# A normalisation of queries and keys that covers two tiles at a time, with its weight applied on ScalarE

## The chip, the cores and the metric

The kernel runs on one core of a Trainium2 chip. The metric is the device time of one execution in microseconds (us); less is better. The median of three runs before the change is 1447.38 us.

## The reference

One encoder layer on 1024 tokens of width 1024: a dilated window attention in three groups of eight heads beside a gated linear recurrence, each behind a gate, then projections and a residual. What matters here is the input projection of the queries and keys and their norm over each head's 64 channels:

```
h = rms_norm(x, norm_w)
z = h @ w_in                                     # [1024, columns], float32
q = rms_norm(qkv_a[:, :, g, 0], q_norm_w[g])     # per token and head, over 64 channels
k = rms_norm(qkv_a[:, :, g, 1], k_norm_w[g])
rms_norm(t, w) = t * rsqrt(mean(t * t, axis=-1) + EPS) * w
```

q and k have 1024 tokens x 3 groups x 8 heads x 64 channels. After it, each group gathers keys and queries by stride (1, 4 or 16 tokens) and does a banded softmax attention.

## The kernel before

**Precision and products.** Each float32 product is three matmuls in a reduced float type on TensorE (PE): operands are split into a rounded high part and a low remainder (`whi`, `wlo` for weights; `hh`, `hl` and the sums `S0h` to `S3l` for the activations), and high x high, low x high and high x low are added in one PSUM bank. ScalarE (ACT) makes the high part, GpSimd (POOL) or VectorE (DVE) the low one.

**Stages.** First the u and v projections (to about 142 us), then the stage this is about, the "blocks" (to about 681 us), then attention, merge, recurrence and output.

**A block.** A block multiplies 256 columns of weights (1024 rows, as four raw tiles of 128 x 512) with all 1024 tokens, by a scheme of seven products instead of eight (`run_quads`, line 449). Its steps, in order, are 11, T1, T2, 21, T3, (11 of the next block), 22, T4; each is 12 matmuls of 128 x 512. Three PSUM banks per block are named `qA` (11, then T2, T3 and T4 added onto it), `qE` (T1, 22) and `qC` (21). Partial results are copied out by ACT: p behind 11, c behind T1, u behind T2; DVE then adds: p is whole behind 21, c behind T3, u behind 22, and the fourth tile is copied behind T4. T3 writes to the bank that u is copied from, so PE can't begin T3 before ACT has copied u. Of the 27 blocks 12 are "qk" blocks, four in each group; they come in pairs, with other blocks (gates, q of the recurrence) between. For a qk block p, c, u and the fourth tile lie in the ring `spare` (7 buffers), for others in `stage`. A tile is 128 channels by 512 tokens; p and u are one half of the tokens, c and the fourth tile the other.

**Rings.** A ring's `get` hands out its buffers in turn; if the next is still in use, the emission first runs waiting tasks until it is free (line 544). The norm has `ny` (4 buffers), `nhi` and `nlo` (2 each); raw weights have `qraw` (6).

**The norm of a tile** (lines 1130 to 1182). As soon as a tile is whole: ACT squares it (`ny`) and copies the square to `nhi`; DVE makes `nlo`; PE sums over the channels of a head with a block matrix of ones (`headones`), two matmuls into a bank `nss`; ACT does Ln, Exp and Square; DVE does three steps in one task (`newton`): a correction from `nss`, the tile times its weight `nqk` and the estimate, and their product, written in the order of the group's stride; then the spare is free, and SP stores the tile to DRAM (`qkD`). 48 tiles, so 96 matmuls. A tile holds two heads of 64 channels.

**What sets the order.** Each engine executes its instructions in program order. That order is made while the program is built: class Plan (line 132) keeps an estimated clock for each engine and each buffer, and class Builder emits a waiting task (`tick`) or a norm product (`burst`) once its inputs are estimated to be there and its ring has room; products of the norm may stand only between two steps. All instructions go through one helper, so every row of the profile has line 58; rows are told apart by tile names. Loads and stores are issued by SP, in its program's order.

Of the kernel before, what the change touches and what calls it, by code (L numbers as in the profile page):

```python
# [8 lines left out]
F32 = mybir.dt.float32  # L9
# [3 lines left out]
AF = mybir.ActivationFunctionType  # L13
# [17 lines left out]
QRAW, SPARE = 6, 7  # L31
LOWS = ("T2", "T4")
# [194 lines left out]
class Builder:  # L227
# [176 lines left out]
    def start_quads(self, ring):  # L404
# [219 lines left out]
def hybrid_block(ctx, tc, a, out):  # L624
# [50 lines left out]
    def block_pages(kind, *at):  # L675
# [11 lines left out]
        return tuple(_dram(wi, (p + 4 * k) * 65536 + 128 * (2 * e + col), [[512, 128], [65536, 4], [1, 128]])  # L687
# [21 lines left out]
    consts.tile([128, 48], F32, name="pad")  # L709
    eps = consts.tile([128, 1], F32, name="eps")  # L710
    half_ones = consts.tile([128, 2], F32, name="half_ones")
    v_.memset(eps, EPS)
    v_.memset(half_ones, 0.0)
    for j in range(2):
        v_.memset(half_ones[64 * j:64 * j + 64, j:j + 1], 1.0)
# [106 lines left out]
    nqk = consts.tile([128, 6], F32, name="nqk")  # L822
# [10 lines left out]
    def bias_tables(p):  # L833
        g_.tensor_scalar(nqk[:, 0:3], nqk[:, 0:3], -0.125 / 128.0, None, op0=OP.mult)
        g_.tensor_scalar(nqk[:, 3:6], nqk[:, 3:6], -1.0 / 128.0, None, op0=OP.mult)
# [155 lines left out]
    for d in range(8):  # L991
# [4 lines left out]
        if d == 3:  # L996
            s_.dma_start(nqk, a["qk_w"])
# [97 lines left out]
    def blocks_start():  # L1095

        if "p" in blk or blk["n"] < 16:
# [13 lines left out]
        v_.tensor_copy(blk["ones"].rearrange("p (j c) -> p j c", j=2),  # L1111
                       half_ones[:, :, None].to_broadcast([128, 2, 64]))
# [1378 lines left out]
```

## Time and profile before

| what | value |
|---|---|
| runs | 1447.38 us (median), 1442.25 and 1447.64 |
| profiled execution | 1447.14 us, span in the profile 1445.4 us |
| granted TensorE clock | 0.999 |
| busy share | PE 99%, DVE 66%, ACT 62%, POOL 24% |
| DMA | 230.52 MB, mean 159 GB/s |

A row of a timeline gives the start in us from the span's beginning, the duration, the engine, the operation with the tiles it writes and reads (`out<-in`), and in brackets how long the engine was idle before it and what released it. A row of a group gives the count, the shortest, median and longest duration in ns, and first and last start. Rows with SPq are DMA issues: the duration there is the issue's.

### The profile page before, as it was taken

Reading aid. Unit: us, or ns where it says so; the run is one execution under the profiler, and the core shown is the slowest. Engines: PE = TensorE matmul, PEld = TensorE weight load, DVE = VectorE, ACT = ScalarE, POOL = GpSimd, SP = SyncE. Lnnn points to the kernel's source line nnn. Section 1 sums busy time; section 2 is a strip of 40 time slices with the busy share of each in tenths; the row PEclk is TensorE's granted clock in tenths of the full one; section 3 lists DMA queues with packets and bytes.
Section 4 is the critical chain, followed back from the end, with each engine's and each line's share of the span. In section 5 each row is a group of like instructions: output and inputs, shape, how many; then the busy total and the mean of one; then the engine's idle time right before and its main releaser. Section 6 shows DMA issues by size and latency. Waiting matters only on the chain. (4 is left out here: it accounts for less than half of the span.)

```text
span 1445.4 us, 23404 instructions
## 1 busy us (share of the span) xinstructions
PE 1430.0 (99%) x8154; PEld 1188.0 (82%) x8154; DVE 959.4 (66%) x1905; ACT 889.0 (62%) x1897; POOL 340.5 (24%) x356
## 2 busy tenths in 40 slices
PE   9999999999999999999999999999999999999998
PEld 8788888888888888888787877788888888888887
DVE  6673678678685788331463546787878787358973
ACT  7743767566575676443587662497777774558461
POOL 0102334454523433334002000032222221001011
PEclk9999999999999999999999999999999999999999
DMA  7746567877643444424758529764444453778665
GB/s 237 184 142 195 170 196 162 197 153 167 151 124 102 98 106 104 123 103 131 263 163 286 162 74 235 226 165 104 127 107 127 109 140 79 207 256 213 188 165 136
DMA packets 224498, 230.52 MB, mean 159 GB/s; under 512 B 73539, under 2 KB 148571, under 8 KB 223868
## 3 DMA queue, kind: packets, MB, share of 16 engines
q1 hardware_dynamic: 209692, 203.67, 46.3%
q0 software_dynamic: 13824, 25.17, 11.4%
q8 instruction: 64, 1.05, 0.3%
q14 instruction: 54, 0.44, 0.1%
q10 hardware_dynamic: 864, 0.19, 0.1%
HBM read 169.03 MB, written 81.43 MB: 173 GB/s over the span
## 5 line engine op out<-in xcount | busy, mean ns | idle before, releaser
L58 POOL TENSOR_TENSOR wlo<-qraw,whi 128x512 fp32r<-128x512 f32 x135 | 192.9, 1435 | 380.2 <-ACT whi L58 299.0
L58 ACT ACTIVATE whi<-qraw 128x512 fp32r<-128x512 f32 x189 | 117.8, 627 | 100.0 <-DVE qraw L58 42.1
L58 DVE TENSOR_TENSOR qraw<-qraw,qraw 128x512 f32<-128x512 f32 x108 | 97.4, 902 | 39.8 <-POOL wlo L58 26.9
L58 PE MATMUL gp<-hh,whi 128*128 128x512 f32 x264 | 109.7, 416 | 0.0
L58 PE MATMUL gp<-hh,wlo 128*128 128x512 f32 x264 | 103.6, 393 | 0.0
L58 PE MATMUL gp<-hl,whi 128*128 128x512 f32 x264 | 103.0, 390 | 0.0
L58 ACT ACTIVATE as<-as,neg 128x192 f32<-128x192 f32 (+2 forms) x192 | 80.4, 424 | 20.1 <-DVE neg L58 20.0
L58 ACT ACTIVATE whi<-raw 128x512 fp32r<-128x512 f32 x92 | 57.2, 627 | 47.7 <-DMA raw<-in_w_in_dram 26.5
L58 PE MATMUL qA<-hh,whi 128*128 128x512 f32 x216 | 84.0, 389 | 0.0
L58 PE MATMUL qA<-hl,whi 128*128 128x512 f32 x216 | 84.0, 389 | 0.0
L58 PE MATMUL qA<-hh,wlo 128*128 128x512 f32 x216 | 84.0, 389 | 0.0
L58 PE MATMUL gp<-whi,hh 128*128 128x512 f32 x192 | 79.1, 412 | 2.4 <-ACT stage L58 2.4
L58 POOL COPY mm<-Bc 128x8 f32<-128x8 f32 x64 | 32.3, 535 | 197.0 <-DVE Bc L58 123.4
L58 PE MATMUL gp<-wlo,hh 128*128 128x512 f32 x192 | 75.4, 393 | 0.3 <-DVE wlo L58 0.3
L58 PE MATMUL gp<-whi,hl 128*128 128x512 f32 x192 | 75.2, 392 | 0.0
L58 DVE CUSTOM_DVE_ANT_0 as<-sc,abias 128x192 f32<-128x192 f32 (+2 forms) x192 | 51.8, 326 | 32.3 <-PE sc L58 25.0
L58 DVE TENSOR_TENSOR wlo<-qraw,whi 128x512 fp32r<-128x512 f32 x54 | 37.3, 692 | 51.2 <-ACT whi L58 51.2
L58 ACT ACTIVATE ny<-ny 128x512 f32<-128x512 f32 x96 | 60.8, 634 | 5.3 <-DMA qkD<-ny 1.6
L58 DVE SCALAR_TENSOR_TENSOR ny<-ny,spare 128x512 f32<-128x512 f32 x48 | 62.2, 1296 | 1.6
L58 PEld LDWEIGHTS gp<-hh,wlo 128*128 128x128 f32 x264 | 49.5, 188 | 11.0
L58 POOL DMA_DIRECT2D wlo<-in_w_in_dram x36 | 31.6, 877 | 113.3 <-ACT wlo L58 97.5
L58 PEld LDWEIGHTS gp<-hh,whi 128*128 128x128 f32 x264 | 49.8, 188 | 8.3
(307 smaller groups left out, 4187.2 us busy)
## 6 DMA issues: line engine op xcount, KB each, us to landing
qraw<-in_w_in_dram SPq DMA_DIRECT2D x108, 256.0 KB, 4.1
raw<-in_w_in_dram SPq DMA_DIRECT2D x84, 256.0 KB, 3.6
qkD<-ny SPq DMA_DIRECT2D x48, 256.0 KB, 3.4
wlo<-in_w_in_dram POOLq DMA_DIRECT2D x36, 256.0 KB, 4.3
sg<-sgD SPq DMA_DIRECT2D x32, 256.0 KB, 2.9
eraw<-wsD SPq DMA_DIRECT2D x32, 256.0 KB, 4.0
sgD<-stage SPq DMA_DIRECT2D x26, 256.0 KB, 2.7
ak<-qkD SPq DMA_DIRECT2D x6, 1024.0 KB, 6.5
```

The source lines that it names most:

```text
L58: got = f(*args, **kw)
```

## The change

A tile now holds 32 channels of four heads instead of 64 of two, and the two tiles of a half (p and u, or c and the fourth) hold the two channel halves of the same four heads. So their squares can be added, and one pair of matmuls (with four blocks of ones, 32 wide) gives the sums for both: 24 pairs of tiles and 48 matmuls. The task for a half begins when both of its tiles are there. Then ACT squares both and multiplies both by their norm weight in place (`Copy` with a scale), DVE adds the squares, and the rest to Ln, Exp, Square is done once. On DVE `newton`, `norm_root` and two `scaled` products are now separate tasks; `scaled` frees its spare. In numbers per two tiles: ACT 8 for 10 instructions, DVE 6 for 8, PE 2 for 4, stores 2 as before. The channel order of the tiles costs more DMAs: each of the 48 raw loads for qk blocks becomes four with pieces of 128 bytes (before one with 512), each 1 MB load of keys or queries in the attention four of 32 partitions. The ring sizes stay.

```diff
+            if isinstance(src, list):
+                for i, x in enumerate(src):
+                    self.p.sp.dma_start(raw[m, b].rearrange("p (d a c) -> p a d c", d=4, a=4)[:, i], x)
+                return
...
-        return tuple(_dram(wi, (p + 4 * k) * 65536 + 128 * (2 * e + col), [[512, 128], [65536, 4], [1, 128]])
+        return tuple([_dram(wi, (p + 4 * k) * 65536 + 256 * e + 32 * col + 64 * i, [[512, 128], [65536, 4], [1, 32]])
+                      for i in range(4)]
...
     def put_qk(g, hv, e):
+        have = {}
+
         def f(half, col, z, mine):
             if not mine:
                 ps, z = z, blk["spare"].get()
                 a_.activation(z, ps, AF.Copy)
-            b.task("act", [z], lambda: squares(g, hv, e, half, col, z), 3, lambda: blk["y"].soon() and blk["hi"].soon())
+            zs = have.setdefault(half, {})
+            zs[col] = z
+            if len(zs) == 2:
+                b.task("act", list(zs.values()), lambda: squares(g, hv, e, half, zs), 3, lambda: blk["y"].soon(2))
         return f
 
-    def squares(g, hv, e, half, col, z):
-        sq, hi = blk["y"].get(), blk["hi"].get()
-        a_.activation(sq, z, AF.Square)
+    def squares(g, hv, e, half, zs):
+        sq, other = blk["y"].get(), blk["y"].get()
+        a_.activation(sq, zs[0], AF.Square)
+        a_.activation(other, zs[1], AF.Square)
+        k = g + 3 * e
+        for col in (0, 1):
+            a_.activation(zs[col], zs[col], AF.Copy, scale=nqk[:, col, k:k + 1])
+        b.task("dve", [sq, other], lambda: sq_sum(g, hv, e, half, zs, sq, other), 3)
+
+    def sq_sum(g, hv, e, half, zs, sq, other):
+        v_.tensor_tensor(sq, sq, other, op=OP.add)
+        blk["y"].done(other)
+        b.task("act", [sq], lambda: sq_high(g, hv, e, half, zs, sq), 3, blk["hi"].soon)
+
+    def sq_high(g, hv, e, half, zs, sq):
+        hi = blk["hi"].get()
         a_.activation(hi, sq, AF.Copy)
-        b.task("dve", [hi], lambda: sq_low(g, hv, e, half, col, z, sq, hi), 3, blk["lo"].soon)
-
-    def sq_low(g, hv, e, half, col, z, sq, hi):
+        b.task("dve", [hi], lambda: sq_low(g, hv, e, half, zs, sq, hi), 3, blk["lo"].soon)
+
+    def sq_low(g, hv, e, half, zs, sq, hi):
         lo = blk["lo"].get()
         v_.tensor_tensor(lo, sq, hi.bitcast(F32), op=OP.subtract)
         blk["y"].done(sq)
-        b.product(0, [lo], lambda: head_sums(g, hv, e, half, col, z, hi, lo), b.gps.soon, merge=False, banks=0)
-
-    def head_sums(g, hv, e, half, col, z, hi, lo):
+        b.product(0, [lo], lambda: head_sums(g, hv, e, half, zs, hi, lo), b.gps.soon, merge=False, banks=0)
+
+    def head_sums(g, hv, e, half, zs, hi, lo):
         ps = b.gps.get(name="nss")
         t_.matmul(ps, blk["ones"], hi, start=True, stop=False)
         t_.matmul(ps, blk["ones"], lo, start=False, stop=True)
         blk["hi"].done(hi)
         blk["lo"].done(lo)
-        b.task("act", [ps], lambda: guess(g, hv, e, half, col, z, ps), 3, lambda: blk["y"].soon(2))
-
-    def guess(g, hv, e, half, col, z, ps):
-        y, y2 = blk["y"].get(), blk["y"].get()
+        b.task("act", [ps], lambda: guess(g, hv, e, half, zs, ps), 3, lambda: blk["y"].soon(3))
+
+    def guess(g, hv, e, half, zs, ps):
+        y, y2, z1 = (blk["y"].get() for _ in range(3))
         a_.activation(y, ps, AF.Ln, scale=1.0 / 64, bias=eps)
         a_.activation(y, y, AF.Exp, scale=-0.5)
         a_.activation(y2, y, AF.Square)
-        b.task("dve", [y2], lambda: newton(g, hv, e, half, col, z, ps, y, y2), 3)
-
-    def newton(g, hv, e, half, col, z, ps, y, y2):
+        b.task("dve", [y2], lambda: newton(g, hv, e, half, zs, ps, y, y2, z1), 3)
+
+    def newton(g, hv, e, half, zs, ps, y, y2, z1):
         v_.scalar_tensor_tensor(y2, ps, 64.0 * EPS, y2, op0=OP.add, op1=OP.mult)
         b.gps.done(ps)
-        k = g + 3 * e
-        v_.scalar_tensor_tensor(z, z, nqk[:, k:k + 1], y, op0=OP.mult, op1=OP.mult)
-        R = (1, 4, 16)[g]
-        res = lambda t: t.rearrange("p (u r) -> p r u", r=R) if R > 1 else t
-        v_.scalar_tensor_tensor(y.rearrange("p (r u) -> p r u", r=R) if R > 1 else y, res(y2), -192.0, res(z),
-                                op0=OP.add, op1=OP.mult)
-        blk["y"].done(y2)
+        b.task("dve", [y, y2], lambda: norm_root(g, hv, e, half, zs, y, y2, z1), 3)
+
+    def norm_root(g, hv, e, half, zs, y, y2, z1):
+        v_.scalar_tensor_tensor(y2, y2, -192.0, y, op0=OP.add, op1=OP.mult)
+        count = [2]
+        for col in (0, 1):
+            b.task("dve", [y2, zs[col]], lambda col=col: scaled(g, hv, e, half, zs[col], y2, y if col else z1, col, count), 3)
+
+    def scaled(g, hv, e, half, z, y2, o, col, count):
+        R = RES[g]
+        n = 512 // R
+        per = lambda t: t.rearrange("p (r u) -> p r u", r=R) if R > 1 else t
+        nat = lambda t: t.rearrange("p (u r) -> p r u", r=R) if R > 1 else t
+        v_.tensor_tensor(per(o), nat(y2), nat(z), op=OP.mult)
         blk["spare"].done(z)
+        count[0] -= 1
+        if count[0] == 0:
+            blk["y"].done(y2)
 
         def out():
-            n = 512 // R
-            dst = qkD[g, hv, 2 * e + col].rearrange("p (r u) -> p r u", r=R)[:, :, n * half:n * half + n]
-            s_.dma_start(dst, y.rearrange("p (r u) -> p r u", r=R))
-            blk["y"].done(y)
-        b.task("sp", [y], out, 1)
+            s_.dma_start(qkD[g, hv, 2 * e + col].rearrange("p (r u) -> p r u", r=R)[:, :, n * half:n * half + n],
+                         o.rearrange("p (r u) -> p r u", r=R))
+            blk["y"].done(o)
+        b.task("sp", [o], out, 1)
...
+    def load_heads(t, g, hv, k):
+        for j in range(2):
+            for c in range(2):
+                s_.dma_start(t[64 * j + 32 * c:64 * j + 32 * c + 32],
+                             qkD[g, hv, k + c].rearrange("(a i d) t -> i d a t", a=2, i=2)[j])
+
     def load_k(g, hv):
         KT[g, hv] = att["k"].get()
-        s_.dma_start(KT[g, hv], qkD[g, hv, 2:4].rearrange("a p t -> p a t"))
+        load_heads(KT[g, hv], g, hv, 2)
         score_tasks(g, hv)
 
     def load_q(g, hv):
         QT[g, hv] = att["q"].get()
-        s_.dma_start(QT[g, hv], qkD[g, hv, 0:2].rearrange("a p t -> p a t"))
+        load_heads(QT[g, hv], g, hv, 0)
```

How ACT's instructions stand in the 4th qk block, at the copy of u, before; in a name the first number is the count within the ring (so `spare_15` takes the buffer of `spare_8`) and the second a running number:

```order
L58 ACTIVATE spare_14_2231<-qE86_2212 128x512
L58 ACTIVATE whi_62_2233<-qraw_23_2160 128x512
L58 ACTIVATE ny_31_2241<-spare_13_2205 128x512
L58 ACTIVATE nhi_11_2242<-ny_31_2241 128x512
L58 ACTIVATE spare_15_2255<-qA83_2120 128x512
L58 ACTIVATE whi_63_2257<-qraw_21_1970 128x512
```

The copy of u, `spare_15`, stands behind the square of the tile that the block before completed with its T4. And now:

```order
L59 ACTIVATE nhi_4_2247<-ny_20_2200 128x512
L59 ACTIVATE nhi_5_2251<-ny_22_2227 128x512
L59 ACTIVATE ny_24_2261<-nss81_2258,eps_82 128x512
L59 ACTIVATE ny_24_2261<-ny_24_2261 128x512
L59 ACTIVATE ny_25_2262<-ny_24_2261 128x512
L59 ACTIVATE spare_15_2274<-qA79_2124 128x512
```

It now stands behind Ln, Exp and Square of a pair. On DVE at the same place, now:

```order
L59 SCALAR_TENSOR_TENSOR ny_25_2262<-nss81_2258,ny_25_2262 128x512
L59 SCALAR_TENSOR_TENSOR ny_25_2262<-ny_25_2262,ny_24_2261 128x512
L59 TENSOR_TENSOR ny_26_2263<-ny_25_2262,spare_8_1936 128x512
L59 TENSOR_TENSOR ny_24_2261<-ny_25_2262,spare_11_2070 128x512
L59 TENSOR_TENSOR spare_12_2155<-qC83_2276,spare_12_2155 128x512
```

The product that reads `spare_8` for the last time is the third step behind that same Square; before, it stood nine DVE rows ahead of the add that follows 21. On PE, between T2 (`qA<-S1`) and 21 (`qC`) of this block, now:

```order
L59 MATMUL qA_2124<-S1l,whi_2006 128x512
L59 MATMUL qA_2124<-S1h,wlo_2007 128x512
L59 MATMUL nss_2258<-nhi_2247,headones 128x512
L59 MATMUL nss_2258<-nlo_2253,headones 128x512
L59 MATMUL nss_2267<-nhi_2251,headones 128x512
L59 MATMUL nss_2267<-nlo_2255,headones 128x512
L59 MATMUL qC_2276<-hh_99,whi_2031 128x512
```

Before, 21 followed T2 directly there, and the norm's matmuls stood around T4. The same order on ACT and DVE stands in the 12th qk block with both pairs between T2 and 21. In the 6th, 8th and 10th block, the copy of u stands behind Ln, Exp and Square too, with one pair of norm matmuls ahead of T2 and one ahead of T3:

```order
L59 ACTIVATE whi_2965<-qraw_2729 128x512
L59 ACTIVATE ny_2973<-nss_2943,eps 128x512
L59 ACTIVATE ny_2973<-ny_2973 128x512
L59 ACTIVATE ny_2974<-ny_2973 128x512
L59 ACTIVATE spare_2982<-qA_2842 128x512
L59 ACTIVATE whi_3001<-qraw_2873 128x512
```

This piece is ACT's in the 6th block: `nss_2943` is the pair ahead of T2, `spare_2982` the copy of u. The order of all matmuls but the norm's is the same before and after.

More of the change, by code (lines that the diff above doesn't have):

```diff
@@ L31 @@
 QRAW, SPARE = 6, 7
+RES = (1, 4, 16)
 LOWS = ("T2", "T4")
@@ L708, in hybrid_block @@
     ident = consts.tile([128, 128], F32, name="ident")
-    consts.tile([128, 48], F32, name="pad")
+    consts.tile([128, 40], F32, name="pad")
     eps = consts.tile([128, 1], F32, name="eps")
-    half_ones = consts.tile([128, 2], F32, name="half_ones")
+    part_ones = consts.tile([128, 4], F32, name="part_ones")
     v_.memset(eps, EPS)
-    v_.memset(half_ones, 0.0)
-    for j in range(2):
-        v_.memset(half_ones[64 * j:64 * j + 64, j:j + 1], 1.0)
+    v_.memset(part_ones, 0.0)
+    for j in range(4):
+        v_.memset(part_ones[32 * j:32 * j + 32, j:j + 1], 1.0)
     a_.dma_start(nw, a["norm_w"])
@@ L820, in hybrid_block @@
     skewD = dr.tile([24, 128 * TABW], F32, name="skewD")
-    nqk = consts.tile([128, 6], F32, name="nqk")
+    nqk = consts.tile([128, 2, 6], F32, name="nqk")
     rb = pre.tile([33, 24], F32, name="rb")
@@ L833, in bias_tables @@
     def bias_tables(p):
[L834 to L835 removed]
+        g_.tensor_scalar(nqk[:, :, 0:3], nqk[:, :, 0:3], -0.125 / 128.0, None, op0=OP.mult)
+        g_.tensor_scalar(nqk[:, :, 3:6], nqk[:, :, 3:6], -1.0 / 128.0, None, op0=OP.mult)
         tbs = pre.tile([96, TABW], F32, name="tbs")
@@ L996, in hybrid_block @@
         if d == 3:
-            s_.dma_start(nqk, a["qk_w"])
+            for c in range(2):
+                for k in range(4):
+                    s_.dma_start(nqk[32 * k:32 * k + 32, c], a["qk_w"][32 * c:32 * c + 32])
             s_.dma_start(rb[0:32, :], a["rel_bias"])
@@ L1110, in blocks_start @@
         a_.preload_act_table_set("natural_log_exp_and_others")
-        v_.tensor_copy(blk["ones"].rearrange("p (j c) -> p j c", j=2),
-                       half_ones[:, :, None].to_broadcast([128, 2, 64]))
+        v_.tensor_copy(blk["ones"].rearrange("p (j c) -> p j c", j=4),
+                       part_ones[:, :, None].to_broadcast([128, 4, 32]))
         b.start_quads(blk["raw"])
@@ L1257, in hybrid_block @@
     QT, KT, BIAS, V, left = {}, {}, {}, {}, {"in": 0, "out": 0, "turned": 0}
+    def load_heads(t, g, hv, k):
+        for j in range(2):
+            for c in range(2):
+                s_.dma_start(t[64 * j + 32 * c:64 * j + 32 * c + 32],
+                             qkD[g, hv, k + c].rearrange("(a i d) t -> i d a t", a=2, i=2)[j])
     def load_k(g, hv):
         KT[g, hv] = att["k"].get()
-        s_.dma_start(KT[g, hv], qkD[g, hv, 2:4].rearrange("a p t -> p a t"))
+        load_heads(KT[g, hv], g, hv, 2)
         score_tasks(g, hv)
```

## The prediction

> **What bounds the kernel now.** I began with the page's first lines (span, busy times), then asked for the busy times of the stretch in which the changed part runs, and for the longest waits of PE.
>
> ```profile
> span 1445.4 us, 23404 instructions
> PE 1430.0 (99%) x8154; PEld 1188.0 (82%) x8154; DVE 959.4 (66%) x1905; ACT 889.0 (62%) x1897; POOL 340.5 (24%) x356
> 145.00:550.00 405.00, 405.00 (x1788) 335.38 (x1787) 296.64 (x358) 262.16 (x448) 168.79 (x133) 1.00 0.59 146
> PE gp L58 <- ACT stage L58: 2.6, 2, 2.4
> PE qA L58 <- ACT stage L58: 0.5, 1, 0.5
> ```
>
> PE is busy for 1430.0 of 1445.4 us. In the third line (window, its length, then busy time and count of PE, PEld, DVE, ACT, POOL, the clock, the DMA share, GB/s) it is busy for all 405 us, at full clock; DVE has 108 us to spare there, ACT 143, and the 16 DMA engines are 59% busy. So a matmul that goes is a gain in full, and any wait of PE that comes is a loss in full: nothing else is waiting to absorb it. The profiled execution took 1447.14 us, 1.7 more than its span, and lies at the median of the runs (1447.38); I add to and take from 1447.14.
>
> **What goes: the norm's matmuls.** All PE rows of the norm, and the place of one pair among its neighbours:
>
> ```profile
> L58 PE MATMUL nss<-nhi,headones x48: 389/389/389, 158.3 to 560.5; 128*128 128x512 f32 x48
> L58 PE MATMUL nss<-nlo,headones x48: 389/389/389, 158.6 to 560.7; 128*128 128x512 f32 x48
> ...
> 158.35 0.39 PE L58 MATMUL nss<-nhi,headones 128*128 128x512 f32 x1
> 158.57 0.39 PE L58 MATMUL nss<-nlo,headones 128*128 128x512 f32 x1
> 158.80 0.39 PE L58 MATMUL qE<-S3h,whi 128*128 128x512 f32 x1
> ```
>
> A matmul is shown as 389 ns long, but two of them take 0.45 us from start to start (158.35 to 158.80): they are pipelined, and the pitch of 0.225 is the price. After the change there are 24 pairs for 48, so 48 x 0.225 = **-10.8 us**. The order of all other matmuls is unchanged, so this does not depend on anything else. ACT loses 48 of 240 instructions, DVE 48 of 192; neither bounds, so I cost that at nothing.
>
> **What comes: waits for a spare buffer.** This is the term that decides. A qk block evacuates its halves into a ring of seven spares, and the norm frees a spare only with its last DVE step. With one tile per norm, each tile started as soon as it was whole; now both tiles of a half must be there, and both pairs of a block start at its end. Spares are held longer, and the instruction order shows the ring run dry. Here is the 4th qk block in the trace of before (ACT, DVE, then PE):
>
> ```profile
> 225.64 0.60 ACT L58 ACTIVATE spare<-qA 128x512 f32<-128x512 f32 x1 [0.44 <-PE qA L58]
> ...
> 228.90 0.58 ACT L58 ACTIVATE spare<-qE 128x512 f32<-128x512 f32 x1
> 229.38 0.62 ACT L58 ACTIVATE whi<-qraw 128x512 fp32r<-128x512 f32 x1
> 230.06 0.64 ACT L58 ACTIVATE ny<-spare 128x512 f32<-128x512 f32 x1
> 230.73 0.64 ACT L58 ACTIVATE nhi<-ny 128x512 fp32r<-128x512 f32 x1
> 231.27 0.58 ACT L58 ACTIVATE spare<-qA 128x512 f32<-128x512 f32 x1
> ...
> 238.07 0.67 ACT L58 ACTIVATE ny<-nss,eps 128x512 f32<-128x512 f32 x1
> 238.77 1.30 ACT L58 ACTIVATE ny<-ny 128x512 f32<-128x512 f32 x2
> ...
> 222.80 0.69 DVE L58 SCALAR_TENSOR_TENSOR ny<-nss,ny 128x512 f32<-128x512 f32 x1 [0.62 <-ACT ny L58]
> 223.41 1.80 DVE L58 SCALAR_TENSOR_TENSOR spare<-spare,nqk,ny 128x512 f32<-128x512 f32 x1
> 225.25 0.69 DVE L58 SCALAR_TENSOR_TENSOR ny<-ny,spare 128x512 f32<-128x512 f32 x1
> ...
> 228.16 0.39 PE L58 MATMUL qA<-S1h,whi 128*128 128x512 f32 x1
> 230.88 0.39 PE L58 MATMUL qC<-hh,whi 128*128 128x512 f32 x1
> 233.60 0.39 PE L58 MATMUL qA<-S2h,whi 128*128 128x512 f32 x1
> ```
>
> Step T2 starts at 228.16, 21 at 230.88, T3 at 233.60. T3 adds onto the bank that the copy at 231.27 (u) reads, so u must be done before it: it is, by 1.7 us, because its spare had come free at 225.94, the end of the DVE row at 225.25. After the change u's copy stands on ACT right behind Ln, Exp and Square of a norm, and its spare is freed by the product that ends that same norm. Count from the start of T2 = 0, with start-to-start times from these rows: ACT 0.51 when independent (229.38 - 228.90 is 0.48, 231.27 - 230.73 is 0.54), DVE 0.61 (223.41 - 222.80), Ln to the end of Square 1.95 (238.07 to 238.77 + 1.30).
>
> The 4th block: ACT's copy of qE starts at 0.74 as now (228.90 - 228.16). Behind it, in the new order, stand whi, two Squares, two scalings, whi, nhi, nhi: eight starts later the first nhi is at 4.3, the second at 4.85, done 0.64 later. DVE's nlo for the second then runs from 5.55 to 6.25. Both norm products now stand between T2 and 21, so 21 starts at 6.3 + 0.45 = 6.75, where it could have started at 2.72 + 4 x 0.225 = 3.62: a wait of 3.1. Ln of the first pair starts near 6.4 and Square ends at 8.35; newton 8.4, root 9.0, product 9.6 to 10.3, u's copy to 11.0. T3 is due at 6.75 + 2.72 = 9.47 and starts at 11.1: 1.6 more. Together 4.7. The 12th qk block has the same order; its product is strided, for which I take the row `ny<-ny,spare` (below: median 1.10 against 0.69): 5.1.
>
> ```profile
> L58 DVE SCALAR_TENSOR_TENSOR ny<-ny,spare x48: 691/1104/2432, 164.1 to 575.7; 128x512 f32<-128x512 f32 x48
> L58 DVE TENSOR_TENSOR nlo<-ny,nhi x48: 673/692/2367, 155.2 to 558.7; 128x512 fp32r<-128x512 f32 x48
> ```
>
> The 6th, 8th and 10th qk blocks: the norm product stands ahead of T2, so only u's copy waits. Before Ln, ACT has the copy of qE and three more, so Ln starts at 2.5, Square ends at 4.5; newton 4.55, root 5.15, strided product 5.75 to 6.85, copy to 7.5, T3 at 7.6. It is due at 2.72 + 0.45 + 2.72 = 5.89: 1.7 each, 5.1 for three. The other six evacuations with this reuse come earlier than needed, or (3rd block) on the edge, and I cost them at nothing: cover of 0 to 2 us. Sum **+14.9**. Bounds: if ACT runs 0.8 earlier everywhere (no wait for DVE's qraw rows behind it), five times 0.8 less, and 3rd block nothing: 11; if POOL holds up one DVE row at each place (nlo and the product reach 2.4 in the rows above, mostly I take 0.5), 17.5.
>
> **What comes: 128-byte pieces.** The 48 loads of raw weights for qk blocks become four DMAs each: 144 more on SP's queue, with 128-byte pieces.
>
> ```profile
> L58 SPq DMA_DIRECT2D qraw<-in_w_in_dram x108: 327/402/1463, 121.6 to 637.8; - x108
>   DVE qraw L58: 12.9, 6
> DMA packets 4128, 0.52 MB, mean 35 GB/s; under 512 B 4128, under 2 KB 4128, under 8 KB 4128
> q1 hardware_dynamic: 4128, 0.52, 23.0%
> ...
> 571.27 0.69 DVE L58 TENSOR_TENSOR qraw<-qraw,qraw 128x512 f32<-128x512 f32 x1 [2.28 <-DMA qraw<-in_w_in_dram]
> 574.56 0.60 ACT L58 ACTIVATE stage<-qA 128x512 f32<-128x512 f32 x1 [0.92 <-DMA sgD<-stage]
> 575.21 0.50 PE L58 MATMUL qA<-S2h,whi 128*128 128x512 f32 x1 [0.54 <-ACT stage L58]
> ```
>
> The 465 to 480 us window holds two stores in 128-byte pieces alone: 4128 packets took 23.0% of 16 engines x 15 us, 13.4 ns each. A tile is 2048 of them: 2048 x 13.4 / 16 = 1.7 us; 48 tiles 82 us, beside the 239 us that are used of 405 now. Bandwidth does not run out even if the old loads are counted too. What shows is lateness: a block's four tiles take 16 issues of 0.402, 6.4 us, where four took 1.6, so the last lands 4.8 later, and a DVE row that waits for it holds up all DVE rows behind it, as the burst holds up the stores behind it on SP. Six such waits are there now, 12.9 us in all, and one reached PE: 2.28 us of wait on DVE at 571.27 became 0.54 on PE, a cover of 1.7. I take one more that reaches PE with the full delay: 4.8 - 1.7 = **+3.1** (none: 0; three: 9.3).
>
> **What comes: keys and queries by quarters.** Each load of 1 MB for the attention becomes four DMAs of 32 partitions. At the first scores:
>
> ```profile
> 686.53 0.37 SPq L58 DMA_DIRECT2D ak<-qkD  x1
> 686.95 0.46 SPq L58 DMA_DIRECT2D aq<-qkD  x1
> 697.04 1.73 PE L58 MATMUL sc<-ak,aq 64*128 64x192 f32 x18 [1.82 <-issue]
> ...
> 700.13 0.43 SPq L58 DMA_DIRECT2D ak<-qkD  x1
> 700.60 0.54 SPq L58 DMA_DIRECT2D aq<-qkD  x1
> ...
> ak<-qkD SPq DMA_DIRECT2D x1, 1024.0 KB, 6.3
> aq<-qkD SPq DMA_DIRECT2D x1, 1024.0 KB, 8.9
> ```
>
> PE waits 1.82 us for them already, so what they lose is lost. Six more issues of 0.42 ahead of the last piece make 2.5 us if nothing covers them, and nothing if the transfers, which take longer than the issues, do: I take 1.5, nearer the upper end since the first piece of the queries now stands behind all four of the keys. The second group's loads (700.13 and 700.60, landing 6.3 and 8.9 us later) do not appear among PE's waits, and I cost later groups at nothing. **+1.5**. The Trainium skill (SBUF — State Buffer, "Can I just issue two DMAs to hit both halves?") speaks against the change here: a transfer over 32 partitions reaches half of the ports, 189 against 328 GB/s at 1 MiB, and transfers side by side do not make up for it. By it this term would be about 5 instead of 1.5, an estimate from that page's figures; no run shown here has such a load.
>
> **Sum.** 1447.14 - 10.8 + 14.9 + 3.1 + 1.5 = 1455.8 us.
>
> **Rivals.** *Not slower: the spares do come free in time.* Place: u's copy in the 4th, 6th, 8th, 10th and 12th block. If ACT and DVE, with 48 instructions less each, run so far ahead that Ln ends before T2 does, the copy is done in time and only the saving is left. It decides at T3: the chain from Ln to u's end, 5.0 us, must start 0.9 after T2's start, not 2.5 (in the 4th and 12th block nhi must come 3.1 earlier). Time: 1447.14 - 10.8 + 1.5 = 1437.8, with late loads 1440.9. For it: DVE idles 27% in this stretch; against it: Ln stands behind the nhi or whi that ACT can't start earlier, since they wait for PE's T1. Chance 0.12.
>
> *Half of the waits.* Only the matmul waits of the 4th and 12th block, or only u's: 7.5 for 14.9, 1448.4. Chance 0.16.
>
> *Half-rate loads.* The 32-partition pieces move at half speed: now 1 MB takes 3.07 us (queries land at 700.60 + 8.9, keys at 700.13 + 6.3), two at half speed 6.1 us more at the first scores in place of 1.5: 1460.4. For it: nothing in the trace; that is the rule cited above. Chance 0.1.
>
> *Three late loads*: 6.2 more, 1462. Chance 0.04. That the saving itself fails is none: a PE that is busy for 405 of 405 us hides nothing.
>
> **How the numbers follow.** The forecast has 0.58, its own range 1449 to 1464 by the bounds of its terms. About 0.5%, 7.2 us, is what a measurement of this kernel can tell from no change: below 1440.1 is faster, above 1454.6 slower. Faster is most of the first rival: 0.11. Within: the rest of it, the second rival, and 0.23 of the forecast (its lower bounds): 0.40. Slower: the rest of the forecast, the half-rate loads and the late ones: 0.49. The range 1444 to 1465 takes in the second rival and the half-rate loads, and leaves out the first rival and the ends.
>
> **What would show it.** In the profile after: 24 + 24 norm matmuls; PE waits in front of `qA<-S2h` put down to ACT's spare, in the 6th, 8th and 10th qk blocks 1 to 2 us each, in the 4th and 12th beside a wait of 3 us in front of `nss` or `qC`; ACT's `spare<-qA` waiting for DVE; PE's busy time down by 10.8 us while the span grows; a wait before the first `sc` of 2 to 5 us. The forecast is wrong if PE stays busy throughout 145 to 550 us; if waits are there but released by `qraw` or `whi`, the loads and not the spares are the price.

## The result and the profile after

The changed kernel takes 1458.46 us (median of four runs, 1455.79 to 1460.08) against 1447.51 for the kernel before (four runs): the ratio is 1.0082 with an interval of 1.0054 to 1.0110, slower by 0.8%. The forecast was 1455.8 in a range of 1444 to 1465. The time lies where it was expected; it is made up differently. The profiled execution of the changed kernel took 1455.79 us, the fastest of its four.

The page's first lines after, then the stretch from 145 to 550 us, then PE's waits:

```profile
span 1453.8 us, 23545 instructions
PE 1426.8 (98%) x8106; PEld 1183.7 (81%) x8106; DVE 916.3 (63%) x1859; ACT 853.6 (59%) x1849; POOL 331.7 (23%) x356
...
145.00:550.00 405.00, 397.32 (x1728) 326.54 (x1727) 256.52 (x312) 227.88 (x398) 162.23 (x133) 0.99 0.65 147
...
PE nss L59 <- ACT nhi L59: 4.9, 2, 2.6
PE o L59 <- ACT apt L59: 4.4, 1, 4.4
...
PE nss L59 <- DVE nlo L59: 2.3, 3, 0.9
PE sc L59 <- issue: 2.0, 1, 2.0
...
PE sc L59 <- DMA aq<-qkD: 1.5, 1, 1.5
...
PE qA L59 <- ACT spare L59: 0.5, 1, 0.5
```

The 48 matmuls are gone (8106 for 8154), but PE is no longer busy for all of the 405 us. The new waits are in two places: in front of `nss` among the blocks, and in the attention (`o`, `sc`). ScalarE and VectorE are less busy than before, so neither became a bound over the stage as a whole.

The 4th qk block on PE, and the stretches around it (window, length, busy time and count of PE, PEld, DVE, ACT, POOL, granted clock, DMA share, GB/s):

```profile
229.99 0.39 PE L59 MATMUL qA<-S1h,wlo 128*128 128x512 f32 x1
232.73 0.50 PE L59 MATMUL nss<-nhi,headones 128*128 128x512 f32 x1 [2.35 <-ACT nhi L59]
234.11 0.79 PE L59 MATMUL nss<-nlo,headones 128*128 128x512 f32 x1 [0.88 <-DVE nlo L59]
234.70 0.63 PE L59 MATMUL nss<-nhi,headones 128*128 128x512 f32 x1
235.13 0.63 PE L59 MATMUL nss<-nlo,headones 128*128 128x512 f32 x1
235.56 0.63 PE L59 MATMUL qC<-hh,whi 128*128 128x512 f32 x1
235.98 0.63 PE L59 MATMUL qC<-hl,whi 128*128 128x512 f32 x1
...
230.48:233.89 3.41, 0.50 (x1) 0.19 (x1) 1.99 (x2) 2.71 (x5) 1.92 (x3) 1.00 0.23 40
233.89:237.31 3.42, 3.20 (x8) 2.52 (x9) 1.10 (x3) 2.30 (x4) 2.02 (x3) 0.50 0.72 102
237.31:240.72 3.41, 3.41 (x16) 2.80 (x15) 2.95 (x5) 1.66 (x4) 0.85 (x1) 1.00 0.96 208
```

PE waits 2.35 + 0.88 = 3.2 us for nhi and nlo. Then the matmuls start 0.43 us apart, not 0.227, until about 237: the granted clock is 0.50 from 233.89 to 237.31. So the wait costs twice, once as a wait and once as slow matmuls behind it, 2.0 us here and 3.2 in the 12th block (there the waits are 2.59 + 0.59, and the clock is at 0.50 for 6.83 us, from 530.85 to 537.68).

ACT and DVE at the copy of u in the same block:

```profile
235.66 1.29 ACT L59 ACTIVATE ny<-ny 128x512 f32<-128x512 f32 x2
236.86 0.58 ACT L59 ACTIVATE spare<-qA 128x512 f32<-128x512 f32 x1
...
237.71 0.69 DVE L59 SCALAR_TENSOR_TENSOR ny<-ny,ny 128x512 f32<-128x512 f32 x1
238.44 1.29 DVE L59 TENSOR_TENSOR ny<-ny,spare 128x512 f32<-128x512 f32 x2
```

The copy begins 1.6 us before the product that was to free its buffer (the row at 238.44). It did not wait for it, so it must have been given another buffer of the ring than the one seven copies back; the trace doesn't name buffers. In the 6th, 8th, 10th and 12th block the copy begins 1.6 us before that product too, and T3 waits in none of the five; in the 6th, 8th and 10th it starts 0.2 us behind the end of the copy, so there was little to spare.

Scores of the attention, after and before (first and last start), and what the DMA engines moved in 7 us ahead of the first score, after (690 to 697 us) and before (688 to 695), and the rows on which ACT stops in the attention, after and before:

```profile
L59 PE MATMUL sc<-ak,aq x512: 217/322/582, 699.3 to 860.1; 64*64 64x64 f32 x85, 64*128 64x192 f32 x54, 64*128 64x256 f32 x32
...
DMA packets 558, 1.71 MB, mean 245 GB/s; under 512 B 100, under 2 KB 100, under 8 KB 558
q1 hardware_dynamic: 558, 1.71, 105.1%
...
699.27 0.56 PE L59 MATMUL sc<-ak,aq 64*128 64x192 f32 x2 [1.96 <-issue]
701.37 4.52 PE L59 MATMUL sc<-ak,aq 64*128 64x192 f32 x30 [1.54 <-DMA aq<-qkD]
784.25 0.63 ACT L59 ACTIVATE whi<-raw 128x512 fp32r<-128x512 f32 x1 [8.47 <-DMA raw<-in_w_in_dram]
```

```profile
L58 PE MATMUL sc<-ak,aq x512: 218/322/480, 697.0 to 849.7; 64*64 64x64 f32 x85, 64*128 64x192 f32 x54, 64*128 64x256 f32 x32
...
DMA packets 991, 2.59 MB, mean 370 GB/s; under 512 B 47, under 2 KB 412, under 8 KB 991
q1 hardware_dynamic: 991, 2.59, 99.7%
...
773.80 0.63 ACT L58 ACTIVATE whi<-raw 128x512 fp32r<-128x512 f32 x1 [3.81 <-DMA raw<-in_w_in_dram]
```

All 16 DMA engines are busy in both, but move 245 GB/s in place of 370. The packets of 4 KB, which are those of keys and queries, show why: in the attention half of them take 0.31 us or more in the changed kernel, and 0.16 before. The scores take 160.8 us from first to last, where they took 152.7.

The sum for the profiled execution (1455.79 against 1447.14, +8.65), from starts on PE. From the first to the last block matmul: 538.4 against 536.5 us, +1.9. That is 48 matmuls fewer (-10.9), waits of 7.7 in place of 0.5 (+7.1), and start-to-start times above 0.227 without a wait, 5.9 in place of 0.3 (+5.7). From there to the last score: 179.5 against 171.2, +8.3. From there to the end 1.9 less, of which 1.1 are waits that were there before and are shorter. The blocks begin 0.2 later, and the execution is 0.2 longer beyond the span. Together 8.7.

Of the 7.7 us of waits 6.4 are those of the 4th and 12th block. The other two are 0.47 us for the copy of u in the first block, and 0.79 in front of `nss` at 207.6 us; VectorE had waited 1.86 us for a raw load just before, but no run settles that this is its cause.

### The profile page after: what moved, and what is told of

Its sections match the earlier page's. It is cut to its first block, busy times and chain, and to the rows that moved or that the text cites. A ratio compares the mean times of both kernels' runs of the same rounds, so it can differ in the third digit from the quotient of the medians.

```text
span 1453.8 us, 23545 instructions
## 1 busy us (share of the span) xinstructions
PE 1426.8 (98%) x8106; PEld 1183.7 (81%) x8106; DVE 916.3 (63%) x1859; ACT 853.6 (59%) x1849; POOL 331.7 (23%) x356
## 4 chain that ended last, share of the span: by engine, by line
PE 84%; DVE 6%; ACT 4%; DMA 3%; SPq 2%; issue 1%; POOL 0%; DVEq 0%; ACTq 0%
PE gp L59 24%; PE qA L59 19%; PE qE L59 9%; PE sA L59 6%; PE qC L59 5%; PE sE L59 4%; PE u L59 3%; PE oB L59 3%; PE o L59 2%; PE sc L59 2%; SPq L59 2%; PE pT L59 2%; DMA aq<-qkD 1%; DVE Bc L59 1%; PE U L59 1%
## 5 line engine op out<-in xcount | busy, mean ns | idle before, releaser
L59 POOL TENSOR_TENSOR wlo<-qraw,whi 128x512 fp32r<-128x512 f32 x135 | 183.6, 1362 | 390.5 <-ACT whi L59 295.9
L59 ACT ACTIVATE spare<-qA 128x512 f32<-128x512 f32 x51 | 30.2, 592 | 57.6 <-PE qA L59 57.5
L59 DVE TENSOR_TENSOR ny<-ny,spare 128x512 f32<-128x512 f32 x48 | 60.6, 1280 | 0.4
```

What stands on the lines that cost most here:

```text
L59: got = f(*args, **kw)
```

## The experiments

All were timed beside the kernel before, in five rounds. "Blocks" is the first to the last block matmul, "scores" from there to the last score, both in the profiled execution; the ratio to the kernel before, which had medians of 1445.8 to 1447.5 beside them, has its 95% interval. Blocks and scores are those of a single execution, which lies up to 3.7 us from the median (weight on VectorE: 1452.72 us). The kernels "changed", "interleaved loads" and "one load" differ only in loads behind the blocks, and yet take 538.4, 539.1 and 541.1 us for them, so a difference of under 3 us in blocks tells little by itself.

| kernel | us | ratio | blocks | scores |
|---|---|---|---|---|
| before | 1447.5 | | 536.5 | 171.2 |
| changed | 1458.46 | 1.0082 (1.0054 to 1.0110) | 538.4 | 179.5 |
| any free spare | 1456.12 | 1.0073 (1.0058 to 1.0088) | 535.8 | 181.3 |
| stores for wide loads | 1539.46 | 1.0630 (1.0602 to 1.0658) | 625.7 | 173.7 |
| weight on VectorE | 1456.45 | 1.0062 (1.0046 to 1.0079) | 532.8 | 181.3 |
| filled wait | 1462.53 | 1.0104 (1.0088 to 1.0120) | 536.8 | 181.0 |
| interleaved loads | 1449.63 | 1.0017 (1.0002 to 1.0031) | 539.1 | 172.1 |
| one load | 1450.05 | 1.0019 (1.0001 to 1.0037) | 541.1 | 169.6 |
| all three | 1448.14 | 1.0012 (0.9995 to 1.0029) | 537.0 | 171.3 |
| all three, 512-byte pieces | 1445.59 | 0.9984 (0.9970 to 0.9999) | 534.4 | 172.2 |
| two of three | 1446.38 | 1.0005 (0.9994 to 1.0016) | 534.1 | 171.3 |
| later sums | 1441.08 | 0.9965 (0.9950 to 0.9980) | 529.9 | 171.6 |
| later sums, further ahead | 1449.32 | 1.0022 (1.0007 to 1.0036) | 540.1 | 170.9 |
| as made, later sums | 1441.00 | 0.9974 (0.9958 to 0.9990) | 530.6 | 171.2 |

### Any free spare

```diff
     def room(self, n=1):
+        if self.tag == "spare":
+            return sum(not f for f in self.flags) + n <= self.bufs
```

(`get` and `when` then take the spare that has been free longest.)

> The builder may take any spare buffer that is free, instead of the one seven copies back; nothing else is changed. Theory 'forced order': both norm products ahead of step 21 in the 4th and 12th qk block are there because the copy of u had to be issued behind the norm that frees one certain spare. With the rule relaxed they move, both PE waits (2.35 + 0.88 and 2.59 + 0.59 us) and the slow matmuls behind them (2.0 and 3.2 us) go, and new short waits at the places where three norm products now stand together may cost 1 to 3 us: 1449 to 1452 us against 1458.5. Rival 'loads': the 128-byte raw loads are what makes the norm late; then the waits stay wherever the products stand, and the time is within 2 us of 1458.5. Rival 'ScalarE queue': four more instructions per pair hold up nhi; the waits shrink by a half at most, 1455.

1456.12 us, where the theory had 1449 to 1452: a miss. The products in the 4th and 12th block moved as the theory said, but three of them then stood together behind the next block's first step, 3 matmuls behind the issue of an nhi; PE waited 1.18, 0.82 and 0.23 us there, and the matmuls behind were slow again; behind three such waits at 544 to 546 us (1.27, 0.82 and 0.22) they were not. Waits in the blocks fell from 7.7 only to 6.9. So the forced place was a place, not the cause: it suggests that what counts is how close a product stands behind its inputs, which the later sums below bear out.

### Stores for wide loads

```diff
-            s_.dma_start(qkD[g, hv, 2 * e + col].rearrange("p (r u) -> p r u", r=R)[:, :, n * half:n * half + n],
+            base = (4 * (2 * g + hv) + 2 * e) * 128 * S + 32 * col * S + n * half
+            s_.dma_start(_dram(qkD, base, [[64 * S, 4], [S, 32], [S // R, R], [1, n]]),
                          o.rearrange("p (r u) -> p r u", r=R))
```

> The stores write the normed tiles in the order in which the attention wants them, so keys and queries are loaded by one DMA of 128 partitions each as before the change (12 loads for 48); the rest is as changed. Theory 'narrow loads': the 6.3 us that are lost behind the blocks come from the 32-partition loads: 3.2 at the first scores (waits of 1.96 and 1.54, then a lowered clock) and the rest where ScalarE waits 8.5 us for raw weights queued behind them. Then the first scores wait 1.8 again, ScalarE's wait falls to about 4, and the time is 1458.5 - 6 = 1452.5 us. Rival: the loss is the shifted start of the attention (2 us later, another meeting with other transfers) and not their width; then at most 1.5 us come back, 1457.

1539.46 us, a miss, and for a reason beside the question. The scores are back (173.7), but the stores, now with an outermost dimension of 4, became so slow that the blocks take 87 us more. From 221 to 231 us, where two such stores are issued at 221 us and a third at 230.8, and little beside them (busy tenths and GB/s in 40 slices, packets; then ACT's wait for a `ny` buffer over the whole execution):

```profile
DMA  8500002605008931274922222222222260232103
GB/s 305 203 0 0 0 8 49 41 0 25 0 8 238 655 66 57 82 303 164 623 98 107 98 98 98 106 98 115 90 74 98 82 188 0 98 123 107 66 0 131
DMA packets 363, 1.18 MB, mean 118 GB/s; under 512 B 60, under 2 KB 68, under 8 KB 324
...
ACT ny L59 <- DMA qkD<-ny: 47.2, 14, 6.7
```

In the row of slices with nothing but 2 the engines are 0.2 busy and move about 98 GB/s: in these 5 us about the 512 KB of the two stores. The Trainium skill (DMA: Bandwidth & Descriptors, "Why a DMA increments its semaphore by 16 and not by 1") says that a DMA uses the largest number of engines, 16 at most, that divides the slowest dimension on both of its sides; four of 16 would be 0.25, an estimate by that rule, and about what the trace shows.

### Weight on VectorE

```diff
-        for col in (0, 1):
-            a_.activation(zs[col], zs[col], AF.Copy, scale=nqk[:, col, k:k + 1])
...
-        v_.tensor_tensor(per(o), nat(y2), nat(z), op=OP.mult)
+        v_.scalar_tensor_tensor(per(o), nat(z), nqk[:, col, k:k + 1], nat(y2), op0=OP.mult, op1=OP.mult)
```

> VectorE applies the norm weight inside its last product (one instruction as before), ScalarE's two scalings per pair are left out; the rest is as changed. Theory 'forced order': the order stays, the two norm products still stand ahead of step 21 in the 4th and 12th qk block, but four instructions of 0.51 us each are gone from the queue ahead of nhi, so the wait of 3.2 us shrinks to about 1.2 at both places, and with a shorter wait the matmuls behind it may stay fast: 4 to 9 us less, 1449 to 1454 us. Rival 'loads': nhi waits for late weights, not for the queue: within 2 us of 1458.5.

The blocks take 532.8 us, 5.6 less: the waits at the 4th and 12th block fell from 3.2 each to 1.9 (0.55 + 1.32) and 1.8 (0.80 + 0.95), and the slow matmuls from 5.9 to 2.1. So the four instructions ahead of nhi were nearly half of that wait; 1.2 had been expected to be left. The time fell less, to 1456.45 (1449 to 1454 was expected): the scores took 181.3 here, and the profiled execution was 3.7 us faster than the median.

### Filled wait

```diff
+        at = half == 0 and (g, hv, e) in ((0, 1, 0), (2, 1, 0))
+        if at:
+            for _ in range(11):
+                t_.matmul(ps, blk["ones"], hq[0][0, 0][:, 0], start=True, stop=True)
         t_.matmul(ps, blk["ones"], hi, start=True, stop=False)
```

> As changed, but in the 4th and 12th qk block PE does matmuls on data at hand, into banks that are overwritten or unused, while it would wait: 11 ahead of the first norm matmul and 3 ahead of the second. Theory 'the wait costs twice': the matmuls behind a wait of over 2 us run at half rate (0.43 us for 0.227) until the clock is granted again; with the wait filled the waits' time stays lost but the slow matmuls go: 2.0 + 3.2 us less, 1453 us. Rival: the slow matmuls come from something else there (weights or the other engines); then they stay and the time is 1458.5 or slightly more, for matmuls that reach beyond the wait.

The place behaves as expected; rows at the 4th block:

```profile
231.11 2.65 PE L59 MATMUL nss<-hh,headones 128*128 128x512 f32 x11
...
235.18 0.50 PE L59 MATMUL nss<-nlo,headones 128*128 128x512 f32 x1 [0.21 <-DVE nlo L59]
235.52 0.40 PE L59 MATMUL nss<-nhi,headones 128*128 128x512 f32 x1
235.78 0.50 PE L59 MATMUL nss<-nlo,headones 128*128 128x512 f32 x1
236.12 0.40 PE L59 MATMUL qC<-hh,whi 128*128 128x512 f32 x1
236.35 0.39 PE L59 MATMUL qC<-hl,whi 128*128 128x512 f32 x1
```

`qC` runs at 0.23 from its first matmul, at a granted clock of 1.00, and what was lost to slow matmuls at the two places fell from 5.2 to 1.5 us. So they are a cost of the wait itself. The blocks gain 1.6 only: the 28 added matmuls take 0.3 us more than the waits that they fill, and waits of 0.7 and 1.2 elsewhere are new or longer. The time as a whole, 1462.5, went the wrong way: the stretch behind the attention took 4 us more, with waits of 1.4 and 2.0 us at 901 and 939 us where the changed kernel has one of 1.1; 1.7 us were lost to slow matmuls behind the second. Why the waits grew is not settled.

### Interleaved loads, and one load

```diff
-        for j in range(2):
-            for c in range(2):
-                s_.dma_start(t[64 * j + 32 * c:64 * j + 32 * c + 32],
-                             qkD[g, hv, k + c].rearrange("(a i d) t -> i d a t", a=2, i=2)[j])
+        for c in range(2):
+            s_.dma_start(t[c:128:2], qkD[g, hv, k + c].rearrange("(a p) t -> p a t", a=2))
```

> Keys and queries are loaded by two DMAs each, onto the even and the odd partitions (64 of them, every second one), instead of four onto 32 neighbouring ones; the channels of a head then lie in another order for both alike, which the scores don't see. The rest is as changed. Theory 'narrow loads': a transfer onto 32 neighbouring partitions is slow whatever runs beside it; spread over the whole height it is as fast as before the change. The last score then comes 172 to 174 us behind the last block matmul (179.5 after the change, 171.2 before) and the time is 1458.5 - 6.5 = 1452 us. Rival 'shifted start': the attention is slower because it meets other transfers; then 180 us stay, 1457 us.

The other kernel has one line in this place, `s_.dma_start(t, qkD[g, hv, k:k + 2].rearrange("a p t -> p a t"))`.

> Keys and queries are loaded by one DMA of 128 partitions each as before the change, from tiles in the changed order, so that the scores are taken over channels of different heads; the stores are left alone. Theory 'narrow loads': as with the two interleaved DMAs, within 1.5 us of them, about 1452 us. Rival 'number of DMAs': issues and not the width of the transfers cost the time; then this is 1 to 3 us better than the interleaved loads, which are in turn better than four by as much.

Both have the scores of before (172.1 and 169.6) and are at 1.0017 and 1.0019, faster than the 1452 us that was expected, with blocks no better than in the changed kernel. Ahead of the first score with the interleaved loads (691 to 698 us), and PE's waits in the attention:

```profile
DMA packets 796, 2.31 MB, mean 330 GB/s; under 512 B 72, under 2 KB 276, under 8 KB 796
q1 hardware_dynamic: 796, 2.31, 90.4%
...
PE sc L59 <- issue: 1.0, 1, 1.0
...
PE o L59 <- ACT apt L59: 0.9, 1, 0.9
```

330 GB/s where the changed kernel had 245, and half of the 4 KB packets take 0.16 us again, in both kernels; the 1.5 us for the queries is gone, and the 4.4 us at `o` are 0.9. That is 0.65% of the time, most of the loss, for the spread of the same bytes over the partitions. Two DMAs are as good as one, so their number is not it.

### All three, and with 512-byte pieces

These join the three edits above; the second also loads raw weights as before the change.

> Any free spare may be taken, VectorE applies the norm weight in its product, keys and queries come by two interleaved DMAs. Theory: the three losses are separate (queue ahead of nhi, forced order, narrow loads) and add up; the blocks take 530 to 532 us (538.4 changed, 536.5 before), the attention is as before the change, the time 1440 to 1443 us, below the 1446 to 1447 of before: the saved matmuls show at last. Rival: the waits only move to other places as they did when the spare ring alone was relaxed; blocks of 535 us, 1446 to 1447 us, no faster than before.

> As the kernel with all three, but the raw weights of qk blocks are loaded as before the change, in one DMA with pieces of 512 bytes, so that a tile holds 64 channels of two heads again and the norm adds the wrong channels. It prices the 128-byte pieces. Theory: they keep VectorE waiting but not PE, so this is within 1.5 us of the kernel with all three. Rival 'loads': late weights still reach PE; 3 us or more faster.

1448.14 us, blocks of 537.0: the rival, and a little beyond it. The three products still stand together in the 6th and 21st block of 27 (waits of 1.7 and 0.8 us in front of `nss` at both, slow matmuls behind those in the 21st alone). With 512-byte pieces the blocks take 2.6 us less and the time is 2.5 us lower, near the 3 us of the rival; the two intervals overlap a little, so this size is a rough one. Part of it is seen in one place: the first block's T3 waits 1.03 us for the copy of u in the kernel with 128-byte pieces, and not with 512.

### Two of three

> The norm weight in VectorE's product and the two interleaved loads, with the spare ring as changed. Theory: the two gains add (blocks 533 us as with the weight alone, attention as before the change): 1447 - 536.5 + 533 = 1443 to 1444 us, and the relaxed ring was what cost the kernel with all three its gain. Rival: waits in the blocks move from run to run with the arrival of the 128-byte loads, blocks 536 to 537, 1447 us.

1446.38 us, blocks of 534.1 where 533 was expected: the two gains add, but 2 to 3 us of the time are missing. It is level with before. The relaxed spare ring, which this kernel lacks, gained nothing in the kernel with all three.

### Later sums

```diff
-    b.BACK = 1.2
+    b.BACK, b.SLACK = 1.2, 1.5
...
-        b.task("act", [sq], lambda: sq_high(g, hv, e, half, zs, sq), 3, blk["hi"].soon)
+        b.task("act", [sq], lambda: sq_high(g, hv, e, half, zs, sq), 1, blk["hi"].soon)
```

(and the same priority for `sq_low`).

> All three, and the builder issues a norm product only when its inputs have been there for 1.5 us by its clock (0.6 before), with the high and low parts of the summed squares ahead of other tasks; the products then stand 19 or more matmuls (4.3 us) behind the issue of nhi, and no longer three together. Theory 'products too close behind their inputs': all the waits for nhi and nlo go, the blocks take 526 to 528 us (536.5 - 10.8 and 0 to 2 for u's copies), the time 1437 to 1439 us, 0.6 to 0.7% below before. Rival 'late weights': VectorE's waits for the 128-byte loads hold up whatever is placed; waits come at other steps, 1443 to 1447 us.

1441.08 us, 0.9965 of before, the first that does the whole computation and is faster; the theory had 1437 to 1439. No wait for nhi or nlo is left, and slow matmuls are down to 0.8 us. The edit sets two things, the distance and the priority; they were not tried apart. PE's waits:

```profile
PE qA L59 <- ACT spare L59: 2.2, 1, 2.2
...
PE qA L59 <- ACT stage L59: 1.1, 1, 1.1
...
PE qC L59 <- ACT spare L59: 1.0, 1, 1.0
```

The 2.2 us are again u's copy in the first block; ACT and DVE there:

```profile
154.83 0.63 ACT L59 ACTIVATE whi<-qraw 128x512 fp32r<-128x512 f32 x1 [1.25 <-DMA qraw<-in_w_in_dram]
155.37 0.58 ACT L59 ACTIVATE spare<-qA 128x512 f32<-128x512 f32 x1
...
152.22 0.69 DVE L59 TENSOR_TENSOR qraw<-qraw,qraw 128x512 f32<-128x512 f32 x1 [6.74 <-DMA qraw<-in_w_in_dram]
```

So here the 128-byte loads do reach PE, through ACT's order. The blocks take 529.9 where 526 to 528 was expected; the waits of 2.2, 1.1 and 1.0 us are the rest.

> All three; products issued when their inputs have been there for 2.5 us, and ScalarE and VectorE may be issued 1.8 us ahead of PE by the builder's clock (1.2 before); no product within 37 matmuls of its nhi's issue. Theory: as the kernel before it, 1437 to 1439 us, with no gain over it, since nothing waits there any more. Rival: more work ahead in ScalarE's queue makes the copies that PE waits for (u ahead of T3) late, 1441 to 1445 us.

1449.32 us: worse, by more than its rival said, and in another way than the rival's. PE waits 2.6 and 5.2 us for copies to `stage`, and ACT for a stage buffer whose store stands behind a burst of raw loads on SP:

```profile
359.83 0.60 ACT L59 ACTIVATE stage<-qA 128x512 f32<-128x512 f32 x1 [3.82 <-DMA sgD<-stage]
...
344.37 12.77 SPq L59 DMA_DIRECT2D qraw<-in_w_in_dram  x16
357.24 0.45 SPq L59 DMA_DIRECT2D sgD<-stage  x1
```

Sixteen issues hold SP for 12.8 us; the prediction had allowed 6.4. Distance and lead were changed together here, so which of them drew the burst forward is not shown.

> The change as it was made, ScalarE's scaling included, with any free spare, the interleaved loads and products issued 1.5 us behind their inputs. It asks whether the scaling on ScalarE costs anything once the products stand far enough behind. Theory: no, ScalarE is 60% busy; 1437 to 1440 us. Rival: its 48 scalings still delay copies for PE; 3 us or more above the same kernel with the weight on VectorE.

1441.00 us, level with the weight on VectorE: no cost of ScalarE's scaling is seen once the products stand far enough behind.

## Why the prediction was right, and where it was not

The way was right and so was the size, but the size by luck. Counting the waits for the norm's sums and for u's copy apart, the forecast has five terms: two came as said, two came far smaller, one came five times as large, and a cost that was in no term came beside them. The forecast of +8.7 meets the +8.65 of the profiled execution only because these errors cancel; the medians of the runs moved by 11.0. In the blocks it was the second rival that came true, with the waits for the norm's sums alone (given 0.16), in the attention much of the third.

**The saved matmuls, -10.8.** Right: 24 + 24 in the profile, 10.9 us at the pitch of 0.227. PE's busy time, which was to fall by as much, fell by 3.2 only, since slow matmuls count as busy.

**The waits for the norm's sums, 3.1 in each of the 4th and 12th block.** Right in place and size, 3.23 and 3.18 us, by ACT's queue from the copy of qE to nhi, then nlo. In detail PE waited for nhi and nlo of the first pair; the nlo of the second ended 7.2 us behind T2's start, where the working had 6.25, in time for its product. The weight on VectorE shortened the wait by 1.4 us for four instructions fewer.

**The waits for u's copy, 8.7 us in five blocks.** Wrong: none of these came. The step that failed is the premise, in the text ahead of the prediction too, that a spare takes the buffer of the one seven copies back. The builder's ring forces the order by that rule, but the copy did not wait for that buffer: in all five blocks it began 1.6 us before the product that was to free it. The order put the copy behind Ln and Square, and that alone was early enough.

**What stood in their place in the blocks** was not in the prediction at all: 5.2 us of slow matmuls behind the two waits of 3.2 us. The filled wait shows that they belong to the wait: this is a cost of a wait that the prediction put at nothing. Blocks as a whole: forecast 14.9 + 3.1 = 18.0 over the saving, measured 12.8 (7.1 of waits and 5.7 of slow matmuls).

**Late 128-byte loads, +3.1.** In the changed kernel they are seen to reach PE only in the first block, 0.47 us (the 0.79 us at 207.6 us may be another such place). With the other waits gone they show: 2.5 us between the two kernels with all three, 2.2 in the first block with later sums.

**The attention, +1.5.** Mis-sized: +8.3 to the last score. The step that failed took the loads' own speed as unchanged and only counted issues. The rival with loads at half speed, 6.1 for this term and given 0.1, was the nearest to what happened, though the loss is not at the first scores alone (two waits there, +1.4, and a lowered clock) but also behind raw weights that queue after the slow loads: ACT's 8.47 us, where it waited 3.81 before, and PE's 4.4. The interleaved loads settle that the spread over partitions is the cause. The rule of the Trainium skill that the prediction cited (SBUF — State Buffer) spoke for it: 189 against 328 GB/s for one transfer, a ratio of 0.58; here several ran side by side, at 245 against 370, 0.66, and a 4 KB packet took 0.31 us for 0.16.

## What to carry to other kernels

A saving on the bound engine is kept only if nothing that it waits for moves closer: place each product several microseconds behind the issue of its inputs, and where waits leave PE idle for 2 us or so within 3.4, count about as much again for slow matmuls. When tiles are cut in another way, price the transfers that follow from it by their speed, not by their number: which partitions and how large an outermost dimension. Here the same change was 0.8% slower as made and 0.3% faster with its loads spread, its spare rule relaxed and its sums issued later; that the relaxed spare rule is needed for it is not shown. The kernel before had 0.5 us of waits in its blocks, so those edits had next to nothing to gain there without the change.

## What the runs showed of the hardware

- The granted clock was either 1.00 or 0.50, and in each of the fourteen traces it changed only at the ends of stretches of 3.41 us that follow one another without regard to the waits. What counted was how long PE was idle within one such stretch. At a granted clock of 1.00 all 42 stretches with 1.91 us or more of idle PE were followed by one at 0.50, and none of the 5790 with less than 1.82; three lie between, and one of those was followed by 0.50. At 0.50 matmuls of 512 columns start 0.43 us apart, so a busy stretch loses half of its 3.41 us, 1.7. The clock came back behind every stretch at 0.50 with at most 0.36 us idle, and stayed down behind those with 0.60 or more, which is why the 12th block lost more than the 4th. So the same two waits in the 4th block (0.55 and 1.3 us) were followed by a loss of 1.7 us in the kernel with two of three, where they fall into one stretch (first pair of rows), and of 0.1 us with the weight on VectorE, where a boundary parts them (second pair). With later sums the wait of 2.17 us in the first block is parted too, and no slow matmul follows it.

```profile
228.94:232.35 3.41, 1.59 (x6) 0.75 (x4) 3.14 (x2) 2.49 (x5) 3.41 (x5) 1.00 0.31 41
232.35:235.76 3.41, 3.35 (x8) 2.67 (x9) 2.70 (x5) 1.09 (x2) 1.88 (x3) 0.50 0.91 138
...
228.28:231.69 3.41, 2.69 (x11) 1.67 (x9) 2.46 (x3) 2.51 (x6) 2.80 (x3) 1.00 0.06 8
231.69:235.11 3.42, 2.27 (x10) 1.89 (x11) 2.72 (x4) 2.12 (x4) 2.97 (x4) 1.00 0.91 122
```

- The Trainium skill (TensorE: Matmul & The Clock Gate, "Part 1") speaks of an idle window of about 3.4 us that runs freely. The traces agree with its length and that it runs freely, and differ in that such a window need not be idle throughout: 1.91 us of it were always enough here.
- Four loads onto 32 neighbouring partitions each, with what ran beside them, moved 245 GB/s with all DMA engines busy, two onto every second partition 330 in the same place. In the attention half of the 4 KB packets took 0.31 us or more with the first and 0.16 with the second, so the engines' busy share (105 and 90%) does not show the loss.
- Two stores with an outermost dimension of 4 ran at about 98 GB/s together, with the DMA engines 0.2 busy.
